# Layer 0 of a two-layer decoder step on one Trainium2 core: silu by ScalarE's Silu in place of tanh and a VectorE product, and each group's decays worked out once and kept in DRAM

## The chip, the core and the metric

The kernel runs on one core of a Trainium2 chip. A core has five engines, each with its own in-order queue of instructions: TensorE (PE: matmuls; PEld is its weight load, which overlaps the matmul before it), VectorE (DVE), ScalarE (ACT: activation functions, casts, copies out of PSUM), GpSimd (POOL) and SyncE (SP, which here issues all the DMAs). ACT holds one set of function tables at a time; an ACT_TABLE_LOAD instruction puts another set in its place. Matmuls write to PSUM, a small memory of banks; ACT and DVE carry results from there to SBUF. An engine that waits for a semaphore holds up everything behind it in its own queue.

The metric is the device time of one execution in microseconds, the median of several runs.

## The reference, cut to what matters

Layer 0 is a gated DeltaNet mixer: a convolution with silu on queries, keys and values, a chunked delta rule with a decay per head, and a gated RMSNorm whose gate is a silu too.

```python
def causal_conv(u, buf, w):
    ...
    return jax.nn.silu(y), up[:, up.shape[1] - (CONV_W - 1):]

def gdn_chunked(q, k, v, g, beta, S0, chunk):
    ...
    gc = jnp.cumsum(g, axis=-1)
    decay = jnp.exp(jnp.where(causal, gc[..., :, None] - gc[..., None, :], -jnp.inf))
    L = jnp.where(strict, jnp.einsum('nbhik,nbhjk->nbhij', kb, k) * decay, 0.0)
    ...
    sol = lax.linalg.triangular_solve(A, rhs, left_side=True, lower=True, unit_diagonal=True)
    attn = jnp.einsum('nbhik,nbhjk->nbhij', q, k) * decay
    ...

def gdn_mixer(...):
    ...
    q = jnp.repeat(l2norm(qkv[..., :GDN_KEY_DIM]...), rep, axis=2) * (GDN_HEAD_K ** -0.5)
    ...
    o = rmsnorm(o, gn_w) * jax.nn.silu(z.reshape(B, T, GDN_V_HEADS, GDN_HEAD_V))
    return o.reshape(B, T, GDN_VALUE_DIM) @ w_out, S, new_buf
```

The same `decay` enters twice: in L (with keys and keys) and in attn (with queries and keys). Layer 1 is an RWKV-7 mixer, which the change does not touch.

## The kernel before

All tokens (64 of eight sample sequences, 16 meta tokens, 1024 of the prompt) lie side by side as 1104 columns, in three segments of 384, 384 and 336. Layer 0 goes over eight groups j; a group has one query/key head and two value heads h. Its steps are written in the order keys, prep, queries, norm of the group before, sample state, values, gate, recurrence; what then stands on each engine's queue is decided by a scheduler with its own model of times, which mixes the steps of neighbouring groups. A change in one step so moves instructions of others.

**Dense products.** `dense` makes one projection tile of one segment: 24 matmuls (three products of split operands, eight blocks of the contraction) into a PSUM tile of the tag d, of which there are two. In the profile these are dq, dk, dv and dz (query, key, value, gate). The weights come by DMA (wraw), ACT casts the high half (whi) and POOL subtracts the low half (wlo).

**Convolution and silu** (`conv_tile`). ACT copies the PSUM tile to raw and starts cvy with the first tap; DVE adds three taps (L406). Then ACT writes tanh(cvy/2) over raw and DVE forms (tanh + 1) * cvy, L410. That is twice the silu; the factor is taken out further on: 4e-6 for the epsilon 1e-6 in the norms, 0.5 in G.sk and in hgn. fhist and flast are small PE transposes of the history rows, with the DVE copy lasts.

**Gate** (`gdn_gate`). ACT takes tanh of half the PSUM tile (zg), and DVE multiplies with the PSUM tile once more (L707), so the PSUM buffer is free only after DVE.

**Decays** (`decays`). For one group and segment: a DMA spreads the cumulated log decays (drow, in DRAM) over 128 partitions, 384 KB; POOL masks them with affine_select (L566; the sample segment has two more, L571); ACT takes six exponentials of 128x128. It is called twice for the same numbers: into E in `gdn_prep`, into attn in `gdn_scores`.

**Prep** (`gdn_prep`). PE forms key products (fsc), DVE multiplies them into E, DMAs carry blocks of it through DRAM (ltd) to invA, and DVE inverts 32x32 triangles in 62 dependent steps (`inverse32`, invtmp and invT). Results go through DRAM (g_t, g_u) to T1n and TT, and PE, DVE and ACT merge the blocks: products rY with E, products rU, and ACT writes TT. The last rY of a segment is the last reader of its E buffer; there are three.

**Recurrence** (`gdn_recur`). Nine steps of 128 tokens, the two heads side by side: PE S times K, DVE X, PE TT times X, ACT w, PE w with attn and with ktok, DVE S. attn is the score tile times the decays. mktok, mog, fss and msc are transposes and score products on PE around it.

Of the kernel before, what the change touches and what calls it, by code (L numbers as in the profile page):

```python
# [11 lines left out]
ALU = mybir.AluOpType  # L12
# [23 lines left out]
class Builder:  # L36
# [99 lines left out]
    def vectors(self):  # L136
# [35 lines left out]
        nc.vector.tensor_scalar(self.omu, self.pcol["rwkv_mu"], -1.0, 1.0, op0=ALU.mult, op1=ALU.add)  # L172
        self.hgn = t(cp, [128, 1], "hgn")
        nc.vector.tensor_scalar(self.hgn, self.pcol["gdn_norm_w"], 0.5, None, op0=ALU.mult)
        tctx.close()
# [140 lines left out]
    def gates(self, xh, xl):  # L316
# [41 lines left out]

        self.drow = self.dram([8, 9, 2, 128], "drow")
        for j in range(8):  # L360
            nc.sync.dma_start(self.drow[j].rearrange("t h k -> h t k"), c3(gc)[2 * j:2 * j + 2])
# [12 lines left out]
    def conv_tile(self, ft, xh, xl, dst, done=None):  # L374
# [8 lines left out]
        for s, (c0, n) in enumerate(SEGS):  # L383
# [21 lines left out]
            for k in range(1, 4):  # L405
                nc.vector.scalar_tensor_tensor(y[:, 0:wd], raw[:, k:k + wd], cw[k], y[:, 0:wd], op0=ALU.mult, op1=ALU.add)  # L406
            e = raw
            self.act(e[:, 0:wd], y[:, 0:wd], AF.Tanh, scale=0.5)
            d = dst(s)
            silu = lambda d, e, y: nc.vector.scalar_tensor_tensor(d, e, 1.0, y, op0=ALU.add, op1=ALU.mult)  # L410
            if s == 0:
                v8 = lambda q: q[:, 0:88].rearrange("p (b r) -> p b r", r=11)[:, :, 0:8]
                silu(d[:, 0:64].rearrange("p (b r) -> p b r", r=8), v8(e), v8(y))
                silu(d[:, 64:384], e[:, 88:408], y[:, 88:408])
            else:
                silu(d[:, 0:n], e[:, 0:n], y[:, 0:n])
                if n < 384:
                    nc.gpsimd.memset(d[:, n:384], 0.0)
# [138 lines left out]

    def decays(self, j, s, pool, tag, bufs):

        nc = self.nc  # L560
        E = self.t(pool, [128, 3, 2, 128], tag, bufs)
        nc.sync.dma_start(E.rearrange("p t h k -> p (t h k)"),
                          self.drow[j, 3 * s:3 * s + 3].rearrange("(o t) h k -> o (t h k)", o=1).broadcast_to([128, 768]))
        E6 = E.rearrange("p t h k -> p (t h) k")

        nc.gpsimd.affine_select(E6, E6, pattern=[[0, 6], [1, 128]], compare_op=ALU.is_ge, fill=NEG, base=0, channel_multiplier=-1)  # L566
        if s == 0:
            nc.gpsimd.memset(E6[0:64, 0:2, 64:128], NEG)
            for h in (0, 1):
                v = E6[0:64, h, 0:64].rearrange("p (b r) -> p b r", r=8)  # L570
                nc.gpsimd.affine_select(v, v, pattern=[[-8, 8], [0, 8]], compare_op=ALU.is_ge, fill=NEG, base=0, channel_multiplier=1)  # L571
        for tt in range(3):
            for h in (0, 1):
                self.act(E[:, tt, h], E[:, tt, h], AF.Exp, bias=self.col[:, 3 * s + tt, 1, 2 * j + h:2 * j + h + 1])
        return E

    def gdn_scores(self, j, s, G):

        at = self.decays(j, s, self.gp, "attn", 2)
        p = self.ps("m", 1, "sc")  # L580
        for tt in range(3):
            b = slice(128 * tt, 128 * tt + 128)
            self.mm(p[:, b], G.K[s][:, b], G.Q[s][:, b])
        pv = p[:, 0:384].rearrange("p (t k) -> p t k", t=3)
        self.nc.vector.tensor_tensor(at, pv.unsqueeze(2).broadcast_to([128, 3, 2, 128]), at, op=ALU.mult)
        return at

    def gdn_prep(self, j, G):
# [8 lines left out]
        for s in range(3):  # L597
# [6 lines left out]
            for tt in range(3):  # L604
                nc.vector.scalar_tensor_tensor(p[:, 384:512], p[:, 128 * tt:128 * tt + 128], 1.0, self.ident, op0=ALU.mult, op1=ALU.mult,
                                               accum_out=kq[:, 3 * s + tt:3 * s + tt + 1])
            nc.vector.tensor_scalar(kq[:, q3], kq[:, q3], 4e-6, None, op0=ALU.add)
            nc.vector.reciprocal(rec[:, q3], kq[:, q3])
            nc.vector.tensor_tensor(bp[:, q3], col[:, q3, 0, 2 * j:2 * j + 2], rec[:, q3].unsqueeze(2).broadcast_to([128, 3, 2]),
                                    op=ALU.mult)  # L610
            E = self.decays(j, s, fp, "E", 3)
            for tt in range(3):
# [12 lines left out]
        self.rsqrt(rk, kq, fp, "rk")  # L625
        nc.vector.scalar_tensor_tensor(G.sk, rk, 0.5, kq, op0=ALU.mult, op1=ALU.mult)

# [50 lines left out]
    def gdn_values(self, j, G, xh, xl):  # L678
# [5 lines left out]
        for s in range(3):  # L684
            self.square_norms(G.Q[s], G.qeps[:, 3 * s:3 * s + 3])
        nc.vector.tensor_scalar(G.qeps, G.qeps, 4e-6, 128 * RMS_EPS, op0=ALU.add, op1=ALU.mult)
        for h in (0, 1):
# [8 lines left out]
    def gdn_gate(self, j, G, xh, xl):  # L696
# [3 lines left out]
        for h in (0, 1):  # L700
            c = 4096 + (2 * j + h) * 128
            w = self.load_w(self.i["gdn_w_in"][0][:, c:c + 128])
            for s, (c0, n) in enumerate(SEGS):
                p = self.dense(w, 128, xh, xl, s, label="z")
                z = t(gp, [128, 384], "zg", 6)
                self.act(z[:, 0:n], p[:, 0:n], AF.Tanh, scale=0.5)
                nc.vector.scalar_tensor_tensor(z[:, 0:n], z[:, 0:n], 1.0, p[:, 0:n], op0=ALU.add, op1=ALU.mult)  # L707
                G.zg[h][s] = z
# [881 lines left out]
    def layer0(self, top, right, xa, xc):  # L1590
# [17 lines left out]
        self.gates(kh, kl)  # L1608
        for j in range(8):
            G, before = self.gdn_keys(j, kh, kl), G if j else None  # L1610
            if j == 0:
                if QF:
# [11 lines left out]
            self.gdn_sample_read(j, G)  # L1624
            self.gdn_values(j, G, kh, kl)
            if j or not ZF:
                self.gdn_gate(j, G, kh, kl)
# [155 lines left out]
```

## Time and profile before

| | us |
|---|---|
| runs shown, median of 3 | 2455.74 (2452.48 to 2456.87) |
| the profiled execution, whole | 2463.55 |
| its span, first to last instruction | 2461.6 |
| PE busy | 2285.6 |
| DVE busy | 1657.3 |
| ACT busy | 1370.1 |
| POOL busy | 1090.5 |

The span lies inside the execution's time, 1.95 us shorter. Layer 0 takes the first half of it: the first group's keys begin at some 50 us, its recurrence near 170 us, the eighth group's recurrence ends near 1180 us. The mean granted TensorE clock of the execution is 0.972 of full speed. In a group of rows, "idle before" is the time in which the engine stood ahead of these instructions, with what ended it.

### The profile page before, as it was taken

To read this page: it belongs to the slowest core of one execution; us is meant where nothing else is said; L and a number is where in the kernel's file an instruction comes from. 1 tells how busy PE (TensorE), PEld (TensorE's weight loads), DVE (VectorE), ACT (ScalarE), POOL (GpSimd) and SP (SyncE) were. 2 spreads that over 40 slices of the span, in tenths; PEclk is the share of its full clock that TensorE was granted. 3 is DMA by queue.
4 is the path that set the end of the run, shared out by engine and by line. 5 is a ranking of instruction groups with operands and counts; after the bars stand their busy time and mean duration, and the time that the engine had idled before them with its cause. 6 is when DMAs were issued, how large, how long until landed. Compare 5 with 4: busy or idle time off the path is not lost. (4 is left out here: it accounts for less than half of the span.)

```text
span 2461.6 us, 52742 instructions
## 1 busy us (share of the span) xinstructions
PE 2285.6 (93%) x18593; PEld 2053.9 (83%) x18593; DVE 1657.3 (67%) x4364; ACT 1370.1 (56%) x3817; POOL 1090.5 (44%) x1478
## 2 busy tenths in 40 slices
PE   6989999999999999999999999988979999999996
PEld 5888989898988989889899998876758777877885
DVE  6878676876768586843358344788865687667563
ACT  5455546564555564664336465564434577677663
POOL 3435343433444343441315235433357565656653
PEclk9999999999999999999999999999989999999997
DMA  3323333333332424261531556667565443343331
GB/s 109 103 72 99 84 108 84 102 86 85 88 101 66 118 81 106 73 203 57 150 94 42 168 178 168 165 192 179 148 197 166 125 139 107 91 142 89 109 103 49
DMA packets 471939, 284.66 MB, mean 116 GB/s; under 512 B 187481, under 2 KB 457050, under 8 KB 471674
## 3 DMA queue, kind: packets, MB, share of 16 engines
q1 hardware_dynamic: 471674, 281.29, 40.5%
q8 instruction: 147, 2.41, 0.4%
q14 instruction: 118, 0.97, 0.1%
HBM read 200.00 MB, written 81.17 MB: 114 GB/s over the span
## 5 line engine op out<-in xcount | busy, mean ns | idle before, releaser
L86 POOL TENSOR_TENSOR wlo<-wraw,whi 128x512 fp32r<-128x512 f32 x260 | 349.0, 1346 | 369.4 <-ACT whi L82 334.9
L82 ACT CAST whi<-wraw 128x512 fp32r<-128x512 f32 x260 | 160.0, 617 | 162.0 <-PE dq L76 50.6
L76 PE MATMUL d<-xc,whi 128*128 128x384 f32 (+3 forms) x846 | 239.0, 340 | 1.8 <-ACT ev L1145 1.8
L406 DVE SCALAR_TENSOR_TENSOR cvy<-raw,cw,cvy 128x408 f32<-128x408 f32 (+2 forms) x288 | 176.7, 626 | 16.6 <-ACT cvy L62 14.8
L439 DVE TENSOR_TENSOR invtmp<-invA,invT 72x31 f32<-72x31 f32 (+31 forms) x403 | 163.5, 406 | 17.0 <-POOL invT L434 6.4
L441 DVE TENSOR_TENSOR invT<-invT,invtmp 72x31 f32<-72x31 f32 (+31 forms) x403 | 169.0, 419 | 6.4
L76 PEld LDWEIGHTS d<-xc,whi 128*128 128x128 f32 (+1 forms) x846 | 155.5, 191 | 9.6 <-issue 5.3
L76 PE MATMUL dz<-xc,whi 128*128 128x384 f32 (+1 forms) x480 | 149.5, 343 | 0.0
L76 PE MATMUL dv<-xc,whi 128*128 128x384 f32 (+1 forms) x480 | 146.7, 334 | 0.0
L76 PE MATMUL d<-xa,whi 128*128 128x384 f32 (+3 forms) x450 | 139.0, 342 | 3.4 <-ACT xa L82 2.5
L76 PE MATMUL dz<-xa,whi 128*128 128x384 f32 (+1 forms) x416 | 136.8, 350 | 2.9 <-ACT whi L82 2.6
L76 PE MATMUL d<-xc,wlo 128*128 128x384 f32 (+2 forms) x396 | 131.2, 341 | 0.0
L855 POOL TENSOR_SCALAR Sb<-Sb,eglb 128x128 f32<-128x128 f32 x128 | 80.2, 645 | 88.5 <-DMA Sb<-in_state_gdn 23.1
L76 PE MATMUL rA<-rS,AR 128*64 128x128 f32 x512 | 106.8, 291 | 7.4 <-DVE rS L1432 4.4
L76 PE MATMUL rA<-UV,G 128*64 128x64 f32 x1152 | 112.5, 223 | 0.4 <-ACT UV L62 0.4
L76 PEld LDWEIGHTS rA<-UV,G 128*64 128x64 f32 x1152 | 101.9, 139 | 3.2 <-issue 1.4
L76 PE MATMUL dv<-xa,whi 128*128 128x384 f32 (+1 forms) x288 | 99.9, 347 | 0.1
L62 ACT ACTIVATE rX<-rA,rk 64x64 f32<-64x64 f32 x272 | 83.6, 307 | 23.0 <-PE rA L76 17.1
L76 PE MATMUL dz<-xa,wlo 128*128 128x384 f32 (+1 forms) x256 | 89.8, 351 | 5.3 <-POOL wlo L86 5.3
L1432 DVE SCALAR_TENSOR_TENSOR rS<-rA,DC,pre 64x64 f32<-64x64 f32 x256 | 72.2, 282 | 28.2 <-PE rA L76 22.5
L76 PE MATMUL fG<-AR,BK 128*128 128x128 f32 x576 | 86.3, 288 | 4.4 <-DVE G L1366 2.3
L76 PEld LDWEIGHTS dz<-xc,whi 128*128 128x128 f32 x480 | 89.7, 192 | 0.8
(506 smaller groups left out, 7500.1 us busy)
## 6 DMA issues: line engine op xcount, KB each, us to landing
wraw<-in_gdn_w_in SPq DMA_DIRECT2D x96, 256.0 KB
wraw<-in_rwkv_w_rkvz SPq DMA_DIRECT2D x96, 256.0 KB
Sb<-in_state_gdn SPq DMA_DIRECT2D x64, 256.0 KB
wraw<-in_rwkv_w_o SPq DMA_DIRECT2D x48, 256.0 KB
E<-drow SPq DMA_DIRECT2D x24, 384.0 KB
attn<-drow SPq DMA_DIRECT2D x24, 384.0 KB
wraw<-in_gdn_w_out SPq DMA_DIRECT2D x36, 256.0 KB
out_s_gdn<-Sb SPq DMA_DIRECT2D x32, 256.0 KB
```

Source lines behind the costliest of these rows:

```text
L62: return self.nc.scalar.activation(out, in_, func, bias=bias, scale=scale, **kw)
L76: self.nc.tensor.matmul(out, lhsT, rhs, start=start, stop=stop)
L82: nc.scalar.copy(hi, x)
L86: e.tensor_tensor(lo, x, hi.bitcast(F32), op=ALU.subtract)
L406: nc.vector.scalar_tensor_tensor(y[:, 0:wd], raw[:, k:k + wd], cw[k], y[:, 0:wd], op0=ALU.mult, op1=ALU.add)
L439: nc.vector.tensor_tensor(tmp, A[:, j, j + 1:32].unsqueeze(2).broadcast_to([nb, n, m]), Tv[:, j, 0:m].unsqueeze(1).broadcast_to([nb, n, m] ...
L441: nc.vector.tensor_tensor(Tv[:, j + 1:32, 0:m], Tv[:, j + 1:32, 0:m], tmp, op=ALU.subtract)
L855: nc.gpsimd.tensor_scalar(Sb[:, u], Sb[:, u], self.eglb[:, hv, 4 * g + u:4 * g + u + 1], None, op0=ALU.mult)
L1432: nc.vector.scalar_tensor_tensor(S[hs[h], h, :], dS, DC[hs[h], ci:ci + 1], pre[hs[h], hs[h]], op0=ALU.mult, op1=ALU.add)
```

## The change

Four things change, all in layer 0:

- silu of the convolved tiles and of the gate becomes one ACT instruction with the function Silu. L410 and L707 go. For the segment with the sample tokens it is two ACT instructions (64 and 320 columns) in place of one tanh of 408.
- The factors that took out the doubled silu go with it (4e-6 to 1e-6, 0.5 in G.sk, hgn).
- `decays` is called once for a group and segment, for group 0 ahead of its keys and for group j + 1 behind the values of group j. Its result stays in E for `gdn_prep` and is written to a new DRAM array ed.
- `gdn_scores` reads attn from ed, in place of a second pass of mask and exponentials.

The number of ACT_TABLE_LOAD instructions in the program is 5 before and 42 after; nothing in the text of the kernel places them. POOL's masks for attn and 144 exponentials are gone, and SP has 24 more DMAs (ed).

```diff
-        self.hgn = t(cp, [128, 1], "hgn")
-        nc.vector.tensor_scalar(self.hgn, self.pcol["gdn_norm_w"], 0.5, None, op0=ALU.mult)
+        self.hgn = self.pcol["gdn_norm_w"]
...
+        self.ed = self.dram([8, 3, 128, 768], "ed")
...
-            e = raw
-            self.act(e[:, 0:wd], y[:, 0:wd], AF.Tanh, scale=0.5)
             d = dst(s)
-            silu = lambda d, e, y: nc.vector.scalar_tensor_tensor(d, e, 1.0, y, op0=ALU.add, op1=ALU.mult)
             if s == 0:
-                v8 = lambda q: q[:, 0:88].rearrange("p (b r) -> p b r", r=11)[:, :, 0:8]
-                silu(d[:, 0:64].rearrange("p (b r) -> p b r", r=8), v8(e), v8(y))
-                silu(d[:, 64:384], e[:, 88:408], y[:, 88:408])
+                self.act(d[:, 0:64].rearrange("p (b r) -> p b r", r=8),
+                         y[:, 0:88].rearrange("p (b r) -> p b r", r=11)[:, :, 0:8], AF.Silu)
+                self.act(d[:, 64:384], y[:, 88:408], AF.Silu)
             else:
-                silu(d[:, 0:n], e[:, 0:n], y[:, 0:n])
+                self.act(d[:, 0:n], y[:, 0:n], AF.Silu)
...
-    def decays(self, j, s, pool, tag, bufs):
+    def decays(self, j, s):
...
-        E = self.t(pool, [128, 3, 2, 128], tag, bufs)
+        E = self.t(self.fp, [128, 3, 2, 128], "E", 3)
...
+        nc.sync.dma_start(self.ed[j, s], E.rearrange("p t h k -> p (t h k)"))
         return E
...
-        at = self.decays(j, s, self.gp, "attn", 2)
+        at = self.t(self.gp, [128, 3, 2, 128], "attn", 2)
+        self.nc.sync.dma_start(at.rearrange("p t h k -> p (t h k)"), self.ed[j, s])
...
-            nc.vector.tensor_scalar(kq[:, q3], kq[:, q3], 4e-6, None, op0=ALU.add)
+            nc.vector.tensor_scalar(kq[:, q3], kq[:, q3], 1e-6, None, op0=ALU.add)
...
-            E = self.decays(j, s, fp, "E", 3)
+            E = G.E[s]
...
-        nc.vector.scalar_tensor_tensor(G.sk, rk, 0.5, kq, op0=ALU.mult, op1=ALU.mult)
+        nc.vector.tensor_tensor(G.sk, rk, kq, op=ALU.mult)
...
-        nc.vector.tensor_scalar(G.qeps, G.qeps, 4e-6, 128 * RMS_EPS, op0=ALU.add, op1=ALU.mult)
+        nc.vector.tensor_scalar(G.qeps, G.qeps, 1e-6, 128 * RMS_EPS, op0=ALU.add, op1=ALU.mult)
...
-                self.act(z[:, 0:n], p[:, 0:n], AF.Tanh, scale=0.5)
-                nc.vector.scalar_tensor_tensor(z[:, 0:n], z[:, 0:n], 1.0, p[:, 0:n], op0=ALU.add, op1=ALU.mult)
+                self.act(z[:, 0:n], p[:, 0:n], AF.Silu)
...
         for j in range(8):
+            if j == 0:
+                E = [self.decays(0, s) for s in range(3)]
             G, before = self.gdn_keys(j, kh, kl), G if j else None
+            G.E = E
...
             self.gdn_values(j, G, kh, kl)
+            if j < 7:
+                E = [self.decays(j + 1, s) for s in range(3)]
             if j or not ZF:
                 self.gdn_gate(j, G, kh, kl)
```

The scheduler makes a new order of it. Three places show how the queues move; the numbers behind the names tell one buffer's use from another's.

ACT at the turn from the fifth group to its recurrence, before: the last gate tiles (zg), the exits of the inverse (TT), the exponentials of the next group's decays (E), and the first w of the recurrence.

```order
L82 CAST whi_9278<-wraw_9276 128x512
L62 ACTIVATE zg_8738<-dz_8713 128x384
L82 CAST whi_9800<-wraw_9798 128x512
L62 ACTIVATE TT_13_123<-rU_8026 64x6x64
L62 ACTIVATE E_9420<-E_9420,gcol_131 128x128 x4
L62 ACTIVATE TT_14_124<-rU_8034 64x6x64
L62 ACTIVATE TT_15_125<-rU_8042 64x6x64
L62 ACTIVATE ktok_8772<-mktok_8770,gcol_131 128x128 x2
L62 ACTIVATE E_9420<-E_9420,gcol_131 128x128 x2
L62 ACTIVATE zg_8766<-dz_8741 128x336
L62 ACTIVATE w_8804<-rA_8800,nbp_7663 128x128
L62 ACTIVATE E_9458<-E_9458,gcol_131 128x128 x6
```

The same place in the changed kernel:

```order
L62 ACT_TABLE_LOAD
L62 ACTIVATE E_8371<-E_8371,gcol_131 128x128 x4
L62 ACTIVATE TT_13_123<-rU_7829 64x6x64
L62 ACTIVATE E_8371<-E_8371,gcol_131 128x128 x2
L62 ACT_TABLE_LOAD
L62 ACTIVATE zg_8544<-dz_8519 128x384
L62 ACTIVATE TT_14_124<-rU_7837 64x6x64
L62 ACT_TABLE_LOAD
L62 ACTIVATE E_8390<-E_8390,gcol_131 128x128 x6
L62 ACTIVATE TT_15_125<-rU_7845 64x6x64
L62 ACTIVATE E_8402<-E_8402,gcol_131 128x128 x6
L62 ACT_TABLE_LOAD
```

All 18 exponentials now stand among the exits of the inverse and ahead of the gate's fifth and sixth tile, whose zg follow the last load with the next weights' casts; the fourth tile's zg stands between. Before, the fifth zg was ahead of all of them, and twelve of them were behind the first w.

ACT in the first group, before:

```order
L62 ACTIVATE raw_589<-cvy_597 128x408
L62 ACTIVATE raw_630<-cvy_633 128x384
L62 ACTIVATE E_899<-E_899,gcol_131 128x128 x4
L62 ACTIVATE cvy_669<-raw_665,cw_401 128x336
L62 ACTIVATE E_899<-E_899,gcol_131 128x128 x2
L62 ACTIVATE zg_728<-dz_703 128x384
L62 ACTIVATE E_937<-E_937,gcol_131 128x128 x6
L62 ACTIVATE E_968<-E_968,gcol_131 128x128 x6
L62 ACTIVATE raw_665<-cvy_669 128x336
L62 ACTIVATE zg_756<-dz_731 128x384
```

And changed, from the second key tile on (a load, two silu of the first key tile, a load and four exponentials stand ahead):

```order
L62 ACT_TABLE_LOAD
L62 ACTIVATE K_601<-cvy_674 128x384
L62 ACT_TABLE_LOAD
L62 ACTIVATE E_557<-E_557,gcol_131 128x128
L62 ACTIVATE cvy_709<-raw_705,cw_401 128x336
L62 ACTIVATE E_557<-E_557,gcol_131 128x128
L62 ACTIVATE E_576<-E_576,gcol_131 128x128 x6
L62 ACT_TABLE_LOAD
L62 ACTIVATE zg_767<-dz_742 128x384
L62 ACT_TABLE_LOAD
L62 ACTIVATE E_588<-E_588,gcol_131 128x128 x6
L62 ACT_TABLE_LOAD
```

The first zg now stands behind four more loads and the second segment's six exponentials; the third key tile's silu and the second zg follow the last load shown.

DVE at the end of the first group's inverse, before: the last steps (invtmp, invT) with the taps and products of the value tile between them.

```order
L410 SCALAR_TENSOR_TENSOR vt_1539<-raw_1525,cvy_1533 128x320
L406 SCALAR_TENSOR_TENSOR cvy_1575<-raw_1572,cw_401,cvy_1575 128x384
L439 TENSOR_TENSOR invtmp_1089<-invA_997,invT_999 72x60
L406 SCALAR_TENSOR_TENSOR cvy_1575<-raw_1572,cw_401,cvy_1575 128x384
L406 SCALAR_TENSOR_TENSOR cvy_1617<-raw_1613,cw_401,cvy_1617 128x336
L441 TENSOR_TENSOR invT_999<-invT_999,invtmp_1089 72x2x30
L585 TENSOR_TENSOR attn_1889<-msc_1900,attn_1889 128x768
L406 SCALAR_TENSOR_TENSOR cvy_1617<-raw_1613,cw_401,cvy_1617 128x336
L410 SCALAR_TENSOR_TENSOR vt_1581<-raw_1572,cvy_1575 128x384
L439 TENSOR_TENSOR invtmp_1092<-invA_997,invT_999 72x31
L692 TENSOR_TENSOR bv_1459<-f_1542,sk_888 128x3x128
L406 SCALAR_TENSOR_TENSOR cvy_1617<-raw_1613,cw_401,cvy_1617 128x336
```

And changed:

```order
L436 TENSOR_TENSOR invtmp_1079<-invA_990,invT_992 72x87
L438 TENSOR_TENSOR invT_992<-invT_992,invtmp_1079 72x3x29
L436 TENSOR_TENSOR invtmp_1082<-invA_990,invT_992 72x60
L438 TENSOR_TENSOR invT_992<-invT_992,invtmp_1082 72x2x30
L436 TENSOR_TENSOR invtmp_1085<-invA_990,invT_992 72x31
L438 TENSOR_TENSOR invT_992<-invT_992,invtmp_1085 72x31
L406 SCALAR_TENSOR_TENSOR cvy_1523<-raw_1515,cw_401,cvy_1523 128x408 x3
L406 SCALAR_TENSOR_TENSOR cvy_1564<-raw_1561,cw_401,cvy_1564 128x384 x2
```

The nine taps of the value tile stand behind the last step of the inverse, and its products are gone.

## The prediction

> **What bounds the kernel now.** I read the page's busy shares first, then the busy time by stage (the windows), then what TensorE (PE) waited for inside layer 0, and only then single rows. The profiled execution took 2463.55 us (span 2461.6, and 1.95 around it); every term below is a change against it.
>
> ```profile
> PE 2285.6 (93%) x18593; PEld 2053.9 (83%) x18593; DVE 1657.3 (67%) x4364; ACT 1370.1 (56%) x3817; POOL 1090.5 (44%) x1478
> ...
> core 0: us, PE busy (x) PEld busy (x) DVE busy (x) ACT busy (x) POOL busy (x), PEclk, DMA share, GB/s
> 60.00:175.00 115.00, 104.13 (x852) 98.50 (x851) 86.63 (x216) 55.79 (x155) 44.73 (x74) 0.94 0.33 89
> 175.00:1080.00 905.00, 872.36 (x7163) 796.86 (x7164) 667.81 (x1973) 505.01 (x1610) 378.61 (x582) 0.99 0.35 94
> 1080.00:1200.00 120.00, 117.02 (x765) 111.97 (x764) 42.52 (x111) 55.89 (x212) 36.25 (x35) 1.00 0.38 115
> ```
>
> The change lies in layer 0. There PE is busy for 872.4 of 905 us in the long middle stretch (seven groups of heads, some 120 us each), 104.1 of 115 in the first group, 117.0 of 120 in the last. The matmuls are the same before and after, so their 872.4 us stay. What can be won in the middle is the 32.6 us in which PE stands, and the 1% that the granted clock of 0.99 leaves (9 us). For whom PE stood there:
>
> ```profile
> PE rA L76 <- DVE S L766: 8.3, 16, 1.2
> PE fhist L73 <- DVE lasts L424: 8.2, 7, 1.7
> PE rA L76 <- DVE X L752: 5.5, 8, 1.4
> PE mktok L73 <- DVE zg L816: 3.1, 4, 0.8
> PE rA L76 <- ACT w L62: 2.4, 5, 0.5
> ```
>
> Columns: total us, times, longest. VectorE (DVE) ends 25.1 us of the 32.6, in 35 short waits, ScalarE (ACT) few. So this is a kernel at its PE limit with small DVE-made gaps: the change can gain or lose some tens of us at most.
>
> **What leaves DVE.** The product that completes silu (L410 for the convolved tiles, L707 for the gate):
>
> ```profile
> 175.00:1080.00 905.00, 46.64 (x112) 0.99 0.35 94
> ...
> 175.00:1080.00 905.00, 22.36 (x42) 0.99 0.35 94
> ```
>
> First row L410, second L707 (columns: window, its length, DVE busy and count). 46.6 + 22.4 = 69.0 us leave; DVE's share in the stretch falls from 667.8/905 = 0.738 to 598.8/905 = 0.662. How far PE's waits follow, no row shows. Bounds: nothing (a wait may be pure latency, PE to DVE to PE) and all 25.1. I let them follow the queueing ratio share/(1 - share), 2.82 before and 1.96 after, 30% less: **-8 us**. The clock loss I let shrink alike, 0.3 x 9: **-3 us** (0 to -9).
>
> **What ACT swaps.** Tanh becomes Silu, one for one on the same tile; 144 exponentials go, since the attention factor is now read back from memory; the sample segment's silu is two instructions in place of one. Table loads rise from 5 to 42 by the program's order.
>
> ```profile
> L62 ACT ACTIVATE zg<-dz 128x384 f32<-128x384 f32 x32 | 15.5, 485 | 12.6 <-PE dz L76 8.8 <-DMA ogd<-zg 3.2
> L62 ACT ACTIVATE attn<-attn,gcol 128x128 f32<-128x128 f32 x144 | 46.7, 391 | 69.5 <-POOL attn L566 67.3 <-POOL attn L571 2.0
> ...
> L566 POOL TENSOR_SCALAR_AFFINE_SELECT attn<-attn 128x768 f32<-128x768 f32 x24 | 35.5, 1479 | 87.9 <-DMA attn<-drow 81.3 <-PE msc L76 6.5
> ...
> 55.87 0.49 ACT L62 ACTIVATE ay<-ay 16x336 f32<-16x336 f32 x1
> 56.38 1.28 ACT L62 ACT_TABLE_LOAD   x1
> 57.67 1.22 ACT L62 ACTIVATE ay<-ay,cvals 16x1104 f32<-16x1104 f32 x1
> ```
>
> No Silu runs before; I price it as the Tanh beside it, 485 ns for 128x384 (bounds: 391, the exponential of a third of the elements, and twice 485). 46.7 us of exponentials leave, 37 loads x 1.28 = 47.4 us come: ACT's total stays. The 67.3 us in which ACT stood for POOL's masking of those factors were off PE's path (PE waits for ACT 2.4 us there), so I take nothing for them, nor for POOL's 35.5 us. A load begins 0.02 us after the activation ahead of it ends, and the next activation starts 0.01 us after the load: 1.28 us is its whole price here. [...]
>
> **The turn from one group to the next.** The four loads of each later group stand here, around the exponentials of the next group's decays, with three exits of the inverse (TT) and two gate evictions (zg) among them.
>
> ```profile
> 925.68 0.34 PE L76 MATMUL dz<-xc,whi 128*128 128x384 f32 x1
> 925.86 0.33 PE L76 MATMUL dz<-xc,wlo 128*128 128x384 f32 x1
> ...
> 931.37 0.91 PE L76 MATMUL rY<-T1n,E 64*64 64x64 f32 x12
> ...
> 932.87 1.61 PE L76 MATMUL rY<-T1n,E 64*64 64x64 f32 x24
> ...
> 935.97 2.31 PE L76 MATMUL rU<-TT,invA 64*64 64x64 f32 x36
> ...
> 932.31 2.51 SPq L562 DMA_DIRECT2D E<-drow  x3
> ...
> 936.04 0.87 POOL L566 TENSOR_SCALAR_AFFINE_SELECT E<-E 128x768 f32<-128x768 f32 x1 [3.05 <-PE fhist L73]
> ...
> 936.91 0.48 ACT L62 ACTIVATE TT<-rU 64x384 f32<-64x384 f32 x1 [0.39 <-PE rU L76]
> 937.30 1.26 ACT L62 ACTIVATE E<-E,gcol 128x128 f32<-128x128 f32 x4
> ...
> 941.70 3.61 ACT L62 ACTIVATE E<-E,gcol 128x128 f32<-128x128 f32 x12
> ```
>
> Count from the end of the first rY (932.3), which frees the E buffer. E's load is issued at once, and its exponentials start 5.0 us later (937.3). ACT now holds everything behind them: four exponentials (to 6.3), TT (6.7), two more (7.3), load (8.6), zg of the gate's fourth tile (9.0), TT (9.4), load (10.7), six (12.5), TT (12.9), six (14.7), load (16.0), zg of the fifth (16.4). PE has meanwhile some 15 matmuls of the fourth gate tile, 24 of the fifth and 24 of the sixth (0.175 us apart, from the first two rows; about 11 us), plus 1.6 + 2.3 us of rY and rU and about 0.9 of transposes and the first rA: 15.8 us. The next dense tile needs the PSUM buffer that the fifth zg frees at 16.4: PE stands 0.6 us, in seven turns **+4 us**. The first load hides in ACT's wait for E. Bounds: 0 (E lands sooner) and 4 us a turn, where E lands 3 us later: 28. The write of the decays waits on SP for the last exponentials (14.7); behind it stands the second half of the query's weights, whose buffer is freed by the key weights' split, no sooner than 16.4: nothing, and if that cover went, PE has three key tiles (some 12 us) before it needs them. The read of the attention factor finds data written a group earlier; DMA is at 0.35: nothing, at worst one late read of the sort that POOL now waits for (81.3 us in 24), on DVE's side.
>
> **The first group.** Here loads and exponentials come on top of each other.
>
> ```profile
> 74.10 1.06 ACT L62 ACTIVATE raw<-cvy 128x408 f32<-128x408 f32 x2 [3.07 <-DVE cvy L406]
> ...
> 77.28 0.47 ACT L62 ACTIVATE zg<-dz 128x384 f32<-128x384 f32 x1
> 77.66 3.61 ACT L62 ACTIVATE E<-E,gcol 128x128 f32<-128x128 f32 x12
> ...
> 81.54 0.48 ACT L62 ACTIVATE zg<-dz 128x384 f32<-128x384 f32 x1
> ...
> 81.25 0.40 PE L76 MATMUL dz<-xa,whi 128*128 128x336 f32 x1
> ...
> 85.27 0.42 PE L76 MATMUL dz<-xa,whi 128*128 128x384 f32 x1
> ...
> 98.00:142.40 44.40, 10.69 (x18) 1.00 0.24 67
> ...
> 142.41 0.30 SPq L636 DMA_DIRECT2D g_t<-invT  x1
> ...
> 148.52 0.37 PE L76 MATMUL rY<-T1n,E 32*32 32x32 f32 x6 [3.96 <-DMA T1n<-g_t]
> ...
> 150.00:160.00 10.00, 10.00 (x169) 9.31 (x165) 7.19 (x17) 3.32 (x9) 0.11 (x1) 0.69 0.36 80
> ```
>
> The first zg moves behind four more loads and six more exponentials: 77.3 + 5.1 + 1.9 = 84.3, so PE's third gate tile starts at 84.7 in place of 81.25; the second zg ends at 90.0 (two more loads, six exponentials), and the fourth tile starts there in place of 85.27: PE loses 4.8 us. But the group's end is set by the 62-step inverse on DVE, for which PE stands 3.96 us at 148.5, with a clock of 0.69 (3 us) behind it. It starts 4.8 us later (the last key tile is late alike), is rid of about 3 us of products, and nine of the 18 taps of the row with 10.69 us move behind it, 5.3 us: it ends at 142.4 + 4.8 - 3 - 5.3 = 139, 3.5 us sooner, while one value tile of PE work (5 us) now lies behind it and not ahead. In all: **0 us**; -6 if PE's wait and its slow clock vanish, +7 if the 4.8 and some clock stay.
>
> **Sum:** -8 - 3 + 4 + 0 = -7 us, 2463.55 to 2456.6. The runs shown have a median of 2455.74, 7.8 below the profiled execution, so the forecast for a median is **2449 us** (-0.3%). A measurement here can tell about 0.2%, 5 us, from no change.
>
> **Rivals.** *PE hides it all.* The 35 waits are latency, DVE's relief buys -2, and the turns cost what I gave, +4: 2453 to 2458. For it: PE at 96%, waits of at most 1.7 us. Against it: fhist waits for a plain copy queued on DVE.
> *The gaps close.* All 25 us of DVE waits and the 9 of clock go, the turn costs nothing: 2422. Against it: PE's order is made anew, with waits of its own.
> *The loads stall PE at the turn* (the other side). If E's exponentials start 3 us later than 5.0, the fifth zg comes at 19.4 and PE stands 3.6 us, with a slow clock behind it as at 150 (1 us here): 7 x 4.6 = 32, less the 11 won: 2477. It decides from 1 us of delay on. For it: a load holds TT, zg and the weights' split alike; in the order before, zg stood ahead of the exponentials. Against it: the first load is hidden, and 5.0 us is this trace's own figure.
> [...]
>
> **Chances.** Forecast (-0.2% to -0.8%) 0.38; gaps close 0.05; PE hides it all 0.26; loads stall 0.27; double price 0.04. So faster by over 0.2%: 0.43, within 0.2%: 0.26, slower: 0.31. The range 2425 to 2480 leaves out the double price, most of "the gaps close" and the worst of the stalls. The likeliest case's own range is 2436 to 2451.
>
> **What would show it.** Right: PE's waits for S, X and lasts fall from 22 us to about 15 in the same stretch; DVE busy there near 599; ACT loads at 1.28 us with nothing beside them; at each turn a PE wait below 1 us for a zg; the first rY of the first group near 144 with a shorter wait. Wrong: PE waits of several us for zg, TT or whi at the turns; a wait for a read of the decays; a first group that ends more than 7 us later; or waits for S and X as long as before, since the new order puts them elsewhere.

## The result and the profile after

The changed kernel takes 2481.6 us (median of four runs, 2479.23 to 2485.84) against 2454.4 us before: the ratio is 1.0102 (95% interval 1.0084 to 1.0120), some 25 us. The prediction was 2449 us, 0.3% faster, with a range of 2425 to 2480: wrong in sign, and just outside the range. The profiled execution took 2485.84 us, with a span of 2484.1, 22.5 more than that of before.

First the busy line of the page of the changed kernel:

```profile
PE 2297.0 (92%) x18593; PEld 2063.1 (83%) x18593; DVE 1606.6 (65%) x4187; ACT 1387.5 (56%) x3742; POOL 1048.9 (42%) x1430
```

DVE lost 51 us of work, as meant, and PE, with the same 18593 matmuls, is busy for 11 us more and idle for another 11. To see where, cut the span at a place that every kernel has. In each group's recurrence PE runs the two updates of the sample state (rsw, then msw) back to back, once. The first such pair behind 300 us and the sixth enclose five whole groups of the steady stretch. The table has us in the profiled executions (start of the pair as PE's timeline gives it, the first store of x1T as the end of layer 0):

| | to the first pair | five groups | rest of layer 0 | the rest |
|---|---|---|---|---|
| before | 326.2 | 644.5 | 245.0 | 1245.9 |
| after | 326.7 | 661.8 | 250.1 | 1245.6 |

All of the loss lies in the steady groups: 128.9 us each before, 132.4 after, with 5 us more in the last. For the five groups the windows of before and after (columns as in the prediction) give PE 7.4 us more of idle time, and 10.0 us more of busy time for as many matmuls:

```profile
326.20:970.70 644.50, 622.52 (x5130) 569.79 (x5129) 471.85 (x1400) 360.36 (x1151) 265.48 (x410) 0.99 0.33 91
```

```profile
326.65:988.48 661.83, 632.49 (x5132) 574.77 (x5132) 436.65 (x1290) 367.32 (x1101) 238.91 (x380) 0.99 0.35 98
```

PE's waits in the changed kernel, in the stretch for which the prediction quoted them:

```profile
PE rA L76 <- DVE S L764: 16.0, 18, 1.2
PE dz L76 <- ACT raw L398: 9.7, 6, 1.6
PE rA L76 <- DVE X L750: 4.1, 12, 0.6
PE dk L76 <- ACT zg L62: 2.2, 3, 1.7
...
PE fhist L73 <- DVE lasts L421: 1.4, 1, 1.4
```

The waits for S, X and lasts are 21.5 us in all, where they were 22.0: less for lasts, twice the time for S. New is the second row. Six times, once in each group from the third on, PE's first gate matmul (dz) stands for 1.6 us until ACT has evicted a tile (raw, L398). One of these six, in rows picked from the timeline of the changed kernel (start and length in us; in brackets the idle time before and its releaser):

```profile
778.95 1.27 POOL L86 TENSOR_TENSOR wlo<-wraw,whi 128x512 fp32r<-128x512 f32 x1 [1.06 <-DVE invT L438]
778.98 1.31 DVE L436 TENSOR_TENSOR invtmp<-invA,invT 72x60 f32<-72x60 f32 x1
779.86 0.39 PE L76 MATMUL rA<-w,ktok 128*128 128x128 f32 x2
780.79 0.19 DVE L438 TENSOR_TENSOR invT<-invT,invtmp 72x31 f32<-72x31 f32 x1
781.01 1.96 ACT L632 COPY invA<-invT 72x1024 f32<-72x1024 f32 x1 [2.15 <-DVE invT L438]
781.29 0.49 PE L76 MATMUL rA<-S,K 128*128 128x128 f32 x2 [1.05 <-DVE S L764]
782.88 0.80 ACT L398 COPY raw<-dv 128x384 f32<-128x384 f32 x2
783.40 0.44 PE L76 MATMUL dz<-xa,whi 128*128 128x384 f32 x1 [1.61 <-ACT raw L398]
784.21 0.52 PE L76 MATMUL dz<-xa,wlo 128*128 128x384 f32 x1
784.52 0.52 PE L76 MATMUL dz<-xc,whi 128*128 128x384 f32 x1
...
787.85 0.34 PE L76 MATMUL dz<-xc,wlo 128*128 128x384 f32 x1
788.03 0.33 PE L76 MATMUL dz<-xa,whi 128*128 128x384 f32 x1
```

ACT took its instructions in the order in which they stand. The copy that ends the inverse (L632, from 781.01) stands ahead of the evictions of the last two value tiles (L398, from 782.88); ACT idles 2.15 us for DVE to finish the inverse, copies for 1.96, and only then frees the PSUM buffers that PE needs. And the stall has a tail: from 784.2 to 787.4 the gate matmuls start 0.32 us apart where they start 0.175 apart behind it. Ten matmuls take 3.2 us in place of 1.75, and the granted clock of the window 784.20:787.60 is 0.50. Four of the six stalls have such a tail.

In the kernel before, at this place of a group, the order is the other way round, and the copy is no cover for anything:

```profile
769.93 0.81 ACT L398 COPY raw<-dv 128x384 f32<-128x384 f32 x2
...
773.92 0.62 PE L76 MATMUL dz<-xa,whi 128*128 128x384 f32 x1
...
786.22 0.18 DVE L441 TENSOR_TENSOR invT<-invT,invtmp 72x31 f32<-72x31 f32 x1
786.78 2.06 ACT L633 COPY invA<-invT 72x1024 f32<-72x1024 f32 x1
```

The evictions were done three microseconds before the gate began, and the inverse ended 12 us behind that. (Before had a wait of its own just ahead of this point, for lasts: 1.7 us in every other group, 0.5 in the rest. The change took these away, all but one of 1.4. Behind such a wait, ended at 772.39, the kernel before has a tail too, at a granted clock of 0.50 in 774.00:777.40; in the five groups it is one, where the changed kernel has four. So the five waits for the eviction there, 8.1 us, cover the added idle time, but the tails are no more than some 4 of the 10 us of longer matmuls; no row shown here places the rest.)

### The profile page after: what moved, and what is told of

Same layout as the page of the kernel before. It is cut to its first block, busy times and chain, and to the rows that moved or that the text cites. A ratio compares the mean times of both kernels' runs of the same rounds, so it can differ in the third digit from the quotient of the medians.

```text
span 2484.1 us, 52351 instructions
## 1 busy us (share of the span) xinstructions
PE 2297.0 (92%) x18593; PEld 2063.1 (83%) x18593; DVE 1606.6 (65%) x4187; ACT 1387.5 (56%) x3742; POOL 1048.9 (42%) x1430
## 5 line engine op out<-in xcount | busy, mean ns | idle before, releaser
L436 DVE TENSOR_TENSOR invtmp<-invA,invT 72x31 f32<-72x31 f32 (+31 forms) x403 | 171.7, 426 | 31.3 <-DMA invA<-ltd 16.8
L853 POOL TENSOR_SCALAR Sb<-Sb,eglb 128x128 f32<-128x128 f32 x128 | 81.7, 654 | 94.5 <-DMA Sb<-in_state_gdn 32.8
L62 ACT ACTIVATE w<-rA,nbp 128x128 f32<-128x128 f32 x144 | 52.1, 372 | 111.9 <-PE rA L76 111.6
L76 PEld LDWEIGHTS dz<-xa,whi 128*128 128x128 f32 x416 | 83.2, 202 | 18.8 <-ACT raw L398 10.8
```

Source lines behind the costliest of these rows:

```text
L62: return self.nc.scalar.activation(out, in_, func, bias=bias, scale=scale, **kw)
L76: self.nc.tensor.matmul(out, lhsT, rhs, start=start, stop=stop)
L436: nc.vector.tensor_tensor(tmp, A[:, j, j + 1:32].unsqueeze(2).broadcast_to([nb, n, m]), Tv[:, j, 0:m].unsqueeze(1).broadcast_to([nb, n, m] ...
L853: nc.gpsimd.tensor_scalar(Sb[:, u], Sb[:, u], self.eglb[:, hv, 4 * g + u:4 * g + u + 1], None, op0=ALU.mult)
```

## The experiments

Every ratio is against runs of the kernel before on the same chip, five rounds each, with its 95% interval. "Order theory" is the reading above: the place of one copy on ACT costs most of what was lost. The scheduler makes the order of every engine anew for almost any edit; where two kernels have the same order on all engines, the text says so.

### The parts: e1 to e4

e1 is the changed kernel with one function exchanged; since the function doesn't enter the order, it is the changed kernel without its added table loads. e3 is the same for e2.

```
-                self.act(d[:, 0:n], y[:, 0:n], AF.Silu)
+                self.act(d[:, 0:n], y[:, 0:n], AF.Tanh)
...
-                self.act(z[:, 0:n], p[:, 0:n], AF.Silu)
+                self.act(z[:, 0:n], p[:, 0:n], AF.Tanh)
```

> The changed kernel with Tanh written where Silu stands (silu's product is left out, so q, k, v and the gate are another function). Its instructions stand in the same order on every engine as in the changed kernel, only 37 of the 42 table loads are gone. The order theory (the 26 us come from the places of the instructions: in each of six groups PE waits about 1.05 us for S and then 1.6 us for the eviction of the last value tile, which ACT holds behind the copy that ends the inverse) expects 2470 to 2482 us and the two waits per group as they are. The rival, that the 37 loads cost the time on ACT (47 us of ACT), expects 2450 to 2460 us and those waits gone.

e2 takes of the change's diff the silu part alone (Silu, no product, the constants that go with it), e3 that with Tanh, e4 the decays part alone (`ed`, decays once and ahead, attn read back).

> The silu part alone: Silu on ACT and no product on DVE, but the decays worked out in both places as before. 75 table loads, 33 more than the changed kernel. In its order ACT evicts the value tiles ahead of the copy that ends the inverse. The order theory expects no wait of 1.6 us for that eviction and a time of 2440 to 2465 us; if the loads set the time (1.28 us each, PE behind them), 70 more of them give 2500 us or more; if less work on DVE is worth what I forecast, it is 2443 plus what the loads cost.

> The kernel of e2 with Tanh written where Silu stands (silu's product is left out): the same order on every engine, 70 table loads fewer. It shows what 69 us leave on DVE when nothing is added on ACT. My forecast for that part was -11 us: 2443 us. If the waits for DVE are pure latency: 2452 us. Against e2 it gives the price of 70 loads: under 10 us if they are covered, up to 90 if they are not.

> The decays part alone: a group's decays once, ahead, kept in DRAM, with Tanh and the product on DVE as before, 5 table loads. In its order ACT evicts the value tiles ahead of the copy that ends the inverse. The order theory expects no wait of 1.6 us for that eviction and 2445 to 2462 us. If the trip through DRAM or the earlier decays cost the time, it is 2470 us or more.

| | ratio | interval |
|---|---|---|
| e1, both parts, no added loads | 1.0051 | 1.0032 to 1.0069 |
| e2, silu part | 1.0057 | 1.0036 to 1.0077 |
| e3, silu part, no added loads | 0.9950 | 0.9934 to 0.9967 |
| e4, decays part | 1.0015 | 0.9996 to 1.0034 |

Three prices follow. The silu part without added loads, which is DVE's relief together with the order that comes with it, is worth 0.5%, -12 us (e3). The table loads cost 0.0102 - 0.0051 = 0.5%, 12.5 us for 37 of them, and 0.0057 + 0.0050 = 1.07%, 26 us for 70. The decays part costs nothing that can be told from nought. But -12 and +4 do not make the +12.6 of e1: some 21 us come only where both parts are together. e1's profile holds the same two rows as that of the changed kernel, without the loads:

```profile
PE rA L76 <- DVE S L764: 15.3, 17, 1.2
PE dz L76 <- ACT raw L398: 9.7, 6, 1.6
```

So the loads aren't the cause of these waits; they cost 12.5 us beside them. e2 has no row of dz for raw, as the order theory expected, but its 70 loads put it above the range that it gave.

### The copy taken out of ACT's queue: e5, e6, e9 to e12

e5 alters one line of the changed kernel:

```
-        nc.scalar.copy(Av, Tv.rearrange("p i j -> p j i"))
+        nc.gpsimd.tensor_copy(Av, Tv.rearrange("p i j -> p j i"))
```

> The changed kernel with one line altered: the copy that ends the inverse (invA from invT, 72x1024) is made by GpSimd and not by ACT, so ACT has nothing that waits for the inverse ahead of the eviction of the last value tiles. 30 table loads. The order theory expects PE's wait for that eviction (9.7 us in six groups) and the slow clock behind it gone: 2455 to 2468 us. If the copy's place is not the cause, the time stays at 2475 to 2485 us, or the wait comes back at another instruction.

e6 is the same line in the kernel before, e9 has `nc.vector.tensor_copy` there in the changed kernel, e10 is e5 with Tanh for Silu (the order of e5), e11 and e12 are the line in e4 and in e2.

> The control: the kernel before with the same line altered. There the copy stands behind all value evictions already, so the order theory expects no gain: 2450 to 2460 us. If a copy on GpSimd is worth something by itself (ACT freed of 1 us a group, the inverse ending sooner), it is 2445 us or less, and e5 says nothing on the order.

> The changed kernel with the inverse's last copy on DVE, right behind the inverse there, in place of ACT. ACT again has nothing ahead of the value evictions that waits for the inverse; DVE gets 2 us more in each group and PE waits for DVE. If freeing ACT's queue is what e5 gained, 2448 to 2462 us, with no wait of 1.6 us for the eviction. If e5 gained by GpSimd's part in it or by the chance of its order alone, 2470 us or more.

> The kernel of e5 with Tanh written where Silu stands (silu's product is left out): the same order on every engine, 25 table loads fewer. If loads cost a third of a microsecond each wherever they stand, as e1 and e3 say, 8 to 10 us less than e5: 2439 us. If what they cost lies in the first groups alone (e1), about the same, 2436 to 2440 us; if e5 covers them, 2448 us.

> The decays part alone with the inverse's copy on GpSimd: e5 without Silu (Tanh, and the product on DVE). If the relief of DVE is what e5 wins by (12 us in e3) less its loads, 2450 to 2462 us; if e5 wins by the order that comes with the copy on GpSimd and the decays, 2449 us or less; if the copy on GpSimd does here what it did in e6, 2490 us or more.

> The silu part alone with the inverse's copy on GpSimd: the fourth corner beside e5, e6 and e11. About 70 table loads. Against e6 it gives what silu is worth under that copy, against e5 what the decays in DRAM are worth. If the parts add without the order, it is e2 plus what e6 lost, 2517 us; if the early end of the inverse is what makes the copy harmless (DVE relieved), 2460 to 2475 us.

| copy on | before | decays part | silu part | both | both, no added loads |
|---|---|---|---|---|---|
| ACT | 1 | 1.0015 (e4) | 1.0057 (e2) | 1.0102 | 1.0051 (e1) |
| GpSimd | 1.0168 (e6) | 1.0154 (e11) | 1.0098 (e12) | 0.9977 (e5) | 0.9925 (e10) |
| DVE | | | | 1.0082 (e9) | |

e5 gives back 31 us (0.0102 + 0.0023 = 1.25%) and is below the kernel before. Its waits in the same stretch hold no dz for raw, and S is a third of what it was:

```profile
PE rA L76 <- DVE X L750: 5.9, 10, 0.9
PE rA L76 <- DVE S L764: 5.5, 9, 1.2
```

That is more than the order theory allowed it, and the control spoiled the reading: e6, expected at no change, is 1.7% slower, and e11 is as bad. In e6 the copy takes 2.12 us where ACT took 2.07 in the kernel before, but PE waits elsewhere:

```profile
PE fhist L73 <- DVE lasts L424: 11.2, 7, 1.8
PE rU L76 <- DMA TT<-g_u: 10.9, 16, 2.1
```

The second row is the inverse's way out through DRAM, which came late for the merge. e9 is a miss for the order theory: it, too, has no dz for raw, and its profile a mean granted clock of 0.973 against 0.969 in that of the changed kernel, yet its ratio is 1.0082, with runs from 2467 to 2492; its profile was taken in the fastest of them (2466.9) and can't say why the others are slower. e12 lies between its two cases, and e10 gives the loads 0.5% once more (25 of them, on another chip than e5). So this series showed that the order is worth more than either part of the change, and not that the copy's place is what matters: with each edit the whole order is another.

### A rule of order: e13 to e15

e13's edit adds to the changed kernel a rule of issue order on ACT and nothing else: no new wait, no other engine. (G.inv is the copy that ends the group's inverse, self.evict the eviction of its last value tile.)

```
++            tc.add_manual_dep(G.inv.ins, self.evict.ins.name,
+                              mybir.DependencyInfo(mybir.DependencyClass.NoSync, mybir.DependencyReason.DATA), reason="order")
```

e14 is e13 with Tanh for Silu (the order of e13). e15 is e3 with the rule reversed: the last two evictions behind the copy. The scheduler answers a rule, too, with a new order. Counted by names and shapes, some 370 of ACT's 3700 instructions without loads and 360 of DVE's 4187 stand elsewhere in e13 than in the changed kernel, and e13 has 28 table loads in place of 42; from e3 to e15 it is some 690 of 3844 and 780 of 4187. So these runs price the rule with all that came with it.

> The changed kernel with one rule of order added: on ACT, the copy that ends a group's inverse is issued behind the eviction of that group's last value tile. Nothing waits for anything more. The order theory expects PE's waits for that eviction (9.7 us) gone and most of the 21 us with them: 2456 to 2468 us (ratio 1.000 to 1.005, DVE's relief -12, decays 4, loads 12). If the place of the copy is not the cause, 1.008 or more.

> e13 with Tanh written where Silu stands (silu's product is left out): the same order on every engine, no table loads added. The sum of the parts is -12 + 4, ratio 0.996 to 0.998 (2444 to 2452 us), if the order theory holds. If an order with both parts is slow for another reason, 1.003 or more, as e1 (1.005).

> The kernel of e3 (0.995; silu's product is left out) with the reverse rule: on ACT, the evictions of a group's last two value tiles are issued behind the copy that ends its inverse, as in the changed kernel. The order theory expects the waits of the changed kernel to appear (dz for the eviction, 1 us and more in each group, the slow clock behind some) and 15 to 30 us more than e3: ratio 1.001 to 1.008. If the copy's place does not matter, 0.993 to 0.998.

| | ratio | interval | expected by the order theory |
|---|---|---|---|
| e13 | 1.0025 | 1.0007 to 1.0043 | 1.000 to 1.005 |
| e14 | 0.9962 | 0.9947 to 0.9978 | 0.996 to 0.998 |
| e15 | 1.0143 | 1.0119 to 1.0166 | 1.001 to 1.008 |

e13 and e14 came as expected, and e15 lost more than its range. The rule is worth 1.0102 - 1.0025 = 0.8%, 19 us, when it mends, 14 fewer loads included, and 1.0143 - 0.9950 = 1.9%, 47 us, when it spoils. Free of the loads it is e1 against e14, with 5 loads each: 1.0051 - 0.9962 = 0.9%, 22 us, close to the 21 us that only both parts together had cost. The timeline of e13 at the same point of the group:

```profile
768.90 0.81 ACT L398 COPY raw<-dv 128x384 f32<-128x384 f32 x2
...
771.14 2.08 ACT L632 COPY invA<-invT 72x1024 f32<-72x1024 f32 x1 [1.43 <-DVE invT L438]
771.42 0.49 PE L76 MATMUL rA<-S,K 128*128 128x128 f32 x2 [1.05 <-DVE S L764]
771.67 0.42 PE L76 MATMUL dz<-xa,whi 128*128 128x384 f32 x1
771.92 0.34 PE L76 MATMUL dz<-xa,wlo 128*128 128x384 f32 x1
772.10 0.34 PE L76 MATMUL dz<-xc,whi 128*128 128x384 f32 x1
```

ACT still idles for the inverse (1.43), and nobody minds: the evictions are done, dz starts at once and its matmuls run 0.175 apart. Over e13's five groups the mean granted clock is 1.00 (the row below). The wait of 1.05 for S is still there, so it is no part of what the rule won. The window of e13's five groups, beside that of the changed kernel above:

```profile
327.14:970.42 643.28, 621.81 (x5137) 568.55 (x5136) 440.35 (x1290) 353.88 (x1091) 238.01 (x380) 1.00 0.36 101
```

Of the 18.5 us between the two, PE's idle time is 7.9, and the five waits for the eviction were 8.1. The changed kernel has five stretches of 3.4 us at a granted clock of 0.50 there, four of them the tails; half of their time is 8.5 us, an estimate of what they cost. That leaves some 2 us. The rows so put most of what the rule won at the waits and the tails behind them, though it moved more than one copy. Of e15 the same view of waits as above:

```profile
PE rA L76 <- DVE S L761: 18.8, 21, 2.3
PE dz L76 <- ACT raw L397: 14.3, 7, 2.4
PE rA L76 <- ACT w L62: 5.6, 15, 0.5
```

The waits of the changed kernel, put there by hand, in all seven groups, and a lower clock. A group takes 134.0 us where e3 takes 128.4. Of the 28.3 us in five groups, 12.0 are idle time of PE (32.8 against 20.8; the waits for raw there are 9.5), and some 12 the clock, by the same estimate: 41 us at a granted clock of 0.50 against 17 in e3 (the mean of the five groups is 0.97 against 0.99).

With e14 the sum closes within its intervals: -0.5% (e3) and +0.15% (e4) make 0.9965, and e14 measures 0.9962. The table of places, continued:

| | to the first pair | five groups | rest of layer 0 | the rest |
|---|---|---|---|---|
| e1 | 310.9 | 658.4 | 256.2 | 1247.9 |
| e3 | 313.3 | 641.9 | 248.1 | 1246.1 |
| e5 | 318.5 | 630.1 | 249.9 | 1248.0 |
| e13 | 327.1 | 643.3 | 247.6 | 1244.6 |
| e14 | 317.5 | 643.5 | 247.3 | 1238.4 |
| e15 | 319.4 | 670.2 | 257.5 | 1252.4 |

Kernels of one order that differ in the loads alone (e13 and e14, after and e1) part ahead of the first pair, by 9.6 and 15.8 us; in the five groups behind they differ by -0.2 and 3.5. The other two such pairs go the same way: e2 and e3 by 12.2 and 6.3, e5 and e10 by 8.5 and -3.2. One profile is a rough measure, though: e18, the kernel of e5 once more, has 324.7 and 632.6, 6.2 and 2.5 from e5, and behind layer 0, where nothing differs, e13 and e14 are 6.2 apart. With that noise, the profiles show the loads' cost ahead of the first pair, and none that can be told from nought at the later turns. Windows of e13, then of e14, for the start of the first group (columns as in the prediction):

```profile
60.00:100.00 40.00, 32.74 (x172) 31.45 (x171) 23.54 (x73) 25.43 (x53) 13.54 (x18) 0.83 0.47 138
```

```profile
60.00:100.00 40.00, 35.45 (x205) 34.64 (x205) 25.67 (x76) 17.75 (x50) 14.98 (x19) 0.91 0.51 146
```

Seven loads, ahead of the first group's keys and gate, make ACT busy for 7.7 us more, PE does 33 matmuls fewer in the same 40 us, and its clock is lower (0.83 against 0.91).

### The loads of the first groups: e7, e8, e16 to e18

e7 gives the first two groups Tanh and the product on DVE again (the halves put into the convolution's weights, the function is the same); e8 does so in e5.

```
+                if j < TG:
+                    self.act(z[:, 0:n], p[:, 0:n], AF.Tanh, scale=0.5)
+                    nc.vector.scalar_tensor_tensor(z[:, 0:n], z[:, 0:n], 1.0, p[:, 0:n], op0=ALU.add, op1=ALU.mult)
```

> The changed kernel, with Tanh and the product on DVE in the first two groups of heads (the halves put into the convolution's weights and the norm's weight, so that the function is the same), Silu from the third group on. 26 table loads are left, none before the third group's values but one. From e1 the loads cost 13 us, all of it by the time the second group's inverse is merged, and nothing after: the theory that only the first two groups pay expects 2466 to 2474 us (products back on DVE in two groups included), the waits for the last value tile as they are. If every load costs a third of a microsecond, 16 fewer give 2476 us.

> Both repairs: the inverse's copy on GpSimd (e5) and the first two groups with Tanh (e7). If the two causes are apart, their gains add: 2440 to 2456 us, at or below the kernel before. If the order made for this kernel brings waits of its own, 2460 us or more.

e16 takes out six of the nine loads (not 13, as the expectation has it) that e13 adds ahead of the second group's values, by rules of order (a group's Silu of the key tiles behind the last exponential of its decays, for the first two groups) and Tanh for the first group's gate. e17 has the same on e5, and e18 is e5 once more.

> e13 with two rules added for the first two groups: the Silu of a group's key tiles is issued behind the last exponential of its decays, and the first group's gate tiles take Tanh with the product on DVE (same function). Before the second group's values 3 loads are added to those of the kernel before, in place of 13 (e13). If the loads cost only where ACT has most to do, in the first 330 us, 5 to 9 us less than e13: ratio 0.999 to 1.0005. If they cost the same everywhere, 4 us less: 1.001. If they cost nothing there, 1.0025.

> The same two rules on e5 (the inverse's copy on GpSimd, no rule on its place). If its loads in the first groups cost what they do in e13, 5 to 9 us below e5: ratio 0.994 to 0.996. If the order that comes with it is another, up to 1.002.

> e5 once more, on the chip of e16 and e17: 0.996 to 0.999 if the first measurement holds.

e7 is at 1.0101 (1.0076 to 1.0126), e8 at 1.0004 (0.9985 to 1.0023), e16 at 1.0041 (1.0026 to 1.0055), e17 at 1.0012 (0.9997 to 1.0027), e18 at 0.9983 (0.9965 to 1.0000). None of the first four gained on the kernel it was made from, and e8 and e17 are above e5; e7 and e16 miss what was expected of them, e8 lies at the edge of its range, e17 comes within its second case only, and e18 as expected. e7's first pair comes at 321.3 and e16's at 325.0, 2 to 5 us sooner than in their models, which one profile can't tell from nought. It may be that what holds the Silu back, or brings the product back, costs there what the loads cost; no run shows it. That the 12.5 us of loads can be had back by fewer loads was not shown. Of the kernels that compute the same function, the one of e5 and e18 alone is below the kernel before, by about 0.2%; e18's interval reaches 1.

## Why the prediction was wrong

**What bounds the kernel:** right. PE is at its limit (busy for 622.5 of 644.5 us in the five groups before), the gaps are small (1.7 us at most), and the change moved time by tens of us. But that the matmuls' busy time would stay, since they are the same, did not hold: in the five groups it went from 622.5 to 632.5 us.

**What leaves DVE (-8, and -3 of clock):** right in size by luck, wrong in place. e3 has -12 us, in an order of its own. But its five groups take 641.9 us against 644.5: of the ratio of shares that I took for the steady stretch little came, and the granted clock there is 0.99 in both. The waits for S, X and lasts moved to other instructions instead of shrinking (21.5 us after, 22.0 before). That is what I had named as the sign of being wrong. The gain of e3 lies ahead of the first pair, 313.3 against 326.2, where the first inverse bounds the group: its first rY starts at 136.94 in place of 148.52, with 1.73 us of wait in place of 3.96.

**The first group (0):** right as a sum by luck, wrong in both terms. Relief is worth some 13 us there (e3), the loads 8 to 16 (the four pairs of one order): the first pair came at 326.7 against 326.2. The first rY of the changed kernel starts at 142.93 without a wait, near the 144 that I had named.

**What ACT swaps:** right. The Silu of a gate tile takes 486 ns where Tanh took 485, a load 1283, and the 37 added loads stand one at each change from Silu to the exponential or back:

```profile
L62 ACT ACT_TABLE_LOAD x42 | 53.9, 1283 | 22.2 <-DMA E<-drow 9.5 <-issue 6.1 <-DMA x<-in_x_prompt 6.0
...
L62 ACT ACTIVATE zg<-dz 128x384 f32<-128x384 f32 x32 | 15.5, 486 | 16.5 <-PE dz L76 16.3
```

**The turn (+4):** right within what the runs can tell. PE waits there for zg for 2.2 us in three turns, 1.7 of it in the first; with the order the same, the loads cost the five later turns -3.2 to 6.3 us.

**The step that failed** is a term that the sum put at nothing without a reason: PE waiting for ACT to free a PSUM buffer at the end of the values. I followed the diff's own instructions to their new places, and costed the first group, the turn and the early inverse, each by itself. I did not ask what the early end of the inverse does to the order on ACT at the end of the values: the inverse's exit copy, which began 12.9 us behind the gate's first matmul, now begins 2.4 us ahead of it, and the scheduler put it ahead of two evictions. That its estimate had the copy ready there is my guess, for its estimates are not on record; on the chip DVE was 2 us later, and PE's PSUM buffers were behind it. In place of nothing the runs have some 21 us (e1's excess over e3 and e4; e1 against e14 has 22), and e15 shows that it can be made by hand. A second term was too small: the loads cost 12.5 us, where I had 4 for the turns and 4.8 inside the first group.

**The rivals.** "The loads stall PE at the turn" gave 2477, the nearest number, for a reason that the runs refute: the stall is at another place, and stays when the loads go (e1). "PE hides it all" was right that the waits of the steady stretch are no queue that drains. The double price of a load, 0.04 in the chances and outside the range, is shown by no run: in the changed kernel each of the 42 loads takes 1.28 us, 33 begin within 0.02 us of the end of the ACT instruction ahead (eight of the rest after 1.1 to 2.5 us in which ACT idled), and 39 are followed within 0.02.

## What to carry to other kernels

Where a scheduler lays the order, a change that ends some chain earlier should be read at that chain's exit: list, for each in-order engine, what stands behind the instruction that waits for it, and who waits for that. Here a PSUM eviction stood behind a copy that waited 2 us for another engine, and PE stalled for 1.6; a rule that pins such a copy behind the evictions adds no work and was worth 0.8%, with the order that came with it. And an edit that is to be priced by itself needs its order pinned: of the kernels here that were edited in one line, two got 1.4 and 1.7% slower than their models with the order that came with the line (e11 against e4, and e6).

## What the runs showed of the hardware

The clock fell after short gaps. Behind 1.05 and 1.61 us of idle with half a microsecond of matmuls between, the granted clock was 0.50 for 3.41 us in four of six cases, beginning 0.10 to 1.29 us after the end of the second gap, and the matmuls there started 0.32 us apart and not 0.175. In the other two, behind the same gaps, the granted clock stayed at 1.00 (windows 519.50:522.90 and 1048.60:1052.00), and behind one wait of 1.24 us for S it was 0.50 (1019.70:1023.10; in the 3.40 us ahead PE was busy for 1.90). The longest single gap of the six cases was 1.62 us, and 2.7 us idle of 3.2 came ahead of a half clock four times of six. What decides between the cases no run here shows.

A DVE product of 72x60 that takes 0.21 to 0.22 us in ten of its 16 uses in the changed kernel takes 1.31 in the other six, in all of which GpSimd's subtraction (128x512, 1.27 us) has begun 0.03 us before it: rows 778.95 and 778.98 above, and so in all of the six groups with the stall. It ends 0.07 us after the other, and S, three products later on DVE, is what PE waits 1.05 us for. None of the ten has that subtraction beside it. Why the product is late the rows do not show.

Single executions of one kernel differ by up to 1%, along with the mean granted clock: e4 took 2447.3 us at 0.979 and 2473.3 at 0.968. One profile isn't the kernel: e9's was 14 us below its median.
